# Fifteen up-projection chunks by seven products instead of seven: weight sums on GpSimd, two of four low parts by adding DMAs, the next chunk's first product as filler

## The chip, the cores and the metric

The kernel runs on one core of a Trainium2 chip, in one launch. The metric is the device time of that launch in microseconds (us); lower is better. A core has five engines with a queue of instructions each: TensorE (PE, matmuls; its weight loads are listed as PEld), VectorE (DVE), ScalarE (ACT), GpSimd (POOL) and SyncE (SP, which here only issues DMAs). They run at the same time and wait for one another by semaphores; each works its own queue off in program order. DMAs are issued from the queues of SP and of POOL and are carried out by 16 DMA engines. SBUF is the on-chip memory of 128 partitions; PSUM holds the results of matmuls in eight banks of 128 x 512 float32.

## What is computed

The reference is a trunk of two decoder layers over a stream h of 512 tokens by 1024 features, all in float32. Each layer is an attention and then a gated feed-forward part with a short causal convolution, each between two RMS norms. The change is in the feed-forward part, which both layers have:

```python
def conv_ffn(xn, w_up, cw, cb, w_down):          # xn (1, 512, 1024), w_up (1024, 5632)
    a = xn @ w_up
    T = a.shape[1]
    ap = jnp.pad(a, ((0, 0), (CONV_W - 1, 0), (0, 0)))
    a = sum(ap[:, j:j + T] * cw[j] for j in range(CONV_W)) + cb
    gate, val = jnp.split(a, 2, axis=-1)
    return (jax.nn.gelu(gate, approximate=True) * val) @ w_down
...
        f = conv_ffn(rms_norm(h, g[2]), w_up[l], conv_w[l], conv_b[l], w_down[l])
        h = h + rms_norm(f, g[3])
```

## The kernel before

**Precision.** Every float32 operand is split into a high part (ScalarE copies it into the matmul format float32r) and a low part (what is left, by VectorE's subtraction). A product of two operands is then three matmuls: high x high, high x low, low x high (`mm3`, lines 263 to 265). The low part of a weight is made in one of two ways: by VectorE, `raw - high` (line 62), or by an adding DMA: ScalarE also writes the negated raw (line 56) and a DMA from POOL's queue adds the raw to it (line 77, `accum_op=ALU.add`).

**The up-projection.** `ffn(l, ...)` runs once per layer. The 5632 columns of w_up are taken in 22 chunks; chunk c has 128 columns of the gate and 128 of the value. A plain chunk (`up`) multiplies each of the two by x, transposed (xT, 1024 features by 512 tokens), in 8 steps of 128 features: 2 x 8 x 3 = 48 matmuls of 512 columns. Their results stand in two PSUM banks. `taps` then applies the convolution (ScalarE's Identity, line 592, and two VectorE instructions, lines 593 and 595, for each bank) into a tile bb, `glu` the gelu of the gate (line 613), `product` the product of the two (line 610) into hc, which a DMA from POOL's queue writes to DRAM (line 608).

**Seven products.** The chunks in SEVEN (6, 8, ..., 18) use a scheme in the manner of Strassen and Winograd on a 2 x 2 split: the features in two halves, the tokens in two halves (LO, HI), the gate and the value as the other two. Four weight blocks a11, a12, a21, a22 of 4 x 128 x 128 give the operands A11, A12, A22 and the sums S1 = a21 + a22, S2 = S1 - a11, S3 = a11 - a21, S4 = a12 - S2; sums of the blocks of x (XA, XB) are made once per layer by `sums_in` (line 627 on GpSimd). Seven products of 12 matmuls of 256 columns each, 84 in all, go into the four halves o1 to o4 of the two banks: A11 into o1, S2 into o2, S3 into o3, A12 into o1, S1 into o2, A22 into o3, and S4 into o2. Between them ScalarE copies o1 (s1, line 900) and VectorE makes s12 = o2 + s1 and s17 = o3 + s1 (lines 902, 903), o4 = o2 + s17 (910), o3 += s12 (915) and at the end o2 += s1 (917). Two accesses to one PSUM bank are kept in order even where they touch different halves. The first half of the next, plain chunk stands between A22 and S4.

**Its weights.** `seven_weights(c + 2)` runs as a generator, a step at a time, during chunk c: it takes two raw tiles r0 and r1, makes the four sums on VectorE (lines 656 to 661), four casts on ScalarE (655, 660, 664, 667) and four low parts on VectorE (663, 666, 669, 671).

**What sets the order.** The order in each engine's queue is the program order of the text (`manual_schedule`); nothing is reordered. Tiles come from pools: p8 (16 tiles of 8 KB per partition: operands), p4 (10 of 4 KB: raw weights wraw, weight sums wsum, bb, one gain), p2 (8 of 2 KB: csum, hc) and the eight PSUM banks. The first write into a new tile waits until the last access to the old tile in the same place is done, so a pool also sets when transfers start. `W.load` issues the raw loads on SP's queue (line 46); `W.take` hands raw tiles out, `W.get` gives split ones.

Of the kernel before, what the change touches and what calls it, by code (L numbers as in the profile page):

```python
# [15 lines left out]
T = 512  # L16
# [7 lines left out]
BIG = 3.0e38  # L24


SEVEN = range(6, 19, 2)
ND = NF // 2
LAST = 3

# [66 lines left out]
def trunk_kernel(ctx, tc, x, norm_gains, w_qkv_a, w_o_a, w_q_b, w_o_b, kv_norm, w_kvf, b_f,  # L97
# [164 lines left out]
    def mm3(o, ah, al, bh, bl, first, last, shared=False):  # L262
        pe.matmul(o, ah, bh, start=first, stop=False, skip_group_check=shared)  # L263
        pe.matmul(o, ah, bl, start=False, stop=False, skip_group_check=shared)  # L264
        pe.matmul(o, al, bh, start=False, stop=last, skip_group_check=shared)  # L265
# [317 lines left out]
    def ffn(l, bd, cp, nxt, ahead):  # L583
        hD = tc.dram_tile([NF, 128, T], F32, name="hD")
        sD = tc.dram_tile([ND, 128, 256], F32, name="sD")
        hc = {}

        def taps(c, banks, between=None):
            bb = t4([128, 2, T], name="bb")
            for s, ch in ((0, c), (1, NF + c)):  # L590
                ps = banks[s]
                act.activation(bb[:, s, :], ps, AF.Identity, bias=cp[:, 3, ch:ch + 1], scale=cp[:, 2, ch:ch + 1])  # L592
                dve.scalar_tensor_tensor(bb[:, s, 1:], ps[:, :T - 1], cp[:, 1, ch:ch + 1], bb[:, s, 1:],  # L593
                                         ALU.mult, ALU.add)
                dve.scalar_tensor_tensor(bb[:, s, 2:], ps[:, :T - 2], cp[:, 0, ch:ch + 1], bb[:, s, 2:],  # L595
                                         ALU.mult, ALU.add)
                if s == 0 and between is not None:
                    between()
            return bb

        gated = []
# [1 line left out]
        def product():  # L603

            if gated:
                c, bb = gated.pop()
                if c - 1 in hc:
                    pool.dma_start(hD[c - 1], hc.pop(c - 1))  # L608
                hc[c] = t2([128, T], name="hc")
                dve.tensor_tensor(hc[c], bb[:, 0, :], bb[:, 1, :], ALU.mult)  # L610

        def glu(c, bb):
            act.activation(bb[:, 0, :], bb[:, 0, :], AF.Gelu_apprx_tanh)
            gated.append((c, bb))
# [26 lines left out]

        halves = {}

        def split_pair(pair, src, n=1024):
            act.copy(pair[:, 0, :n], src)
            yield
            dve.tensor_tensor(pair[:, 1, :n], src, pair[:, 0, :n].bitcast(F32), ALU.subtract)

        def seven_weights(c):

            r0, r1 = W.take(2)
            w = [t8([128, 2, 1024], F32R, name="w") for _ in range(4)]
            sa, sb = (t4([128, 1024], name="wsum") for _ in range(2))
            a11, a12, a21, a22 = r0[:, 0:512], r0[:, 512:1024], r1[:, 0:512], r1[:, 512:1024]
            act.copy(w[0][:, 0], r0)
            dve.tensor_tensor(sa[:, 0:512], a11, a21, ALU.subtract)
            dve.tensor_tensor(sb[:, 0:512], a21, a22, ALU.add)
            yield
            dve.tensor_tensor(sa[:, 512:1024], sb[:, 0:512], a11, ALU.subtract)
            act.copy(w[1][:, 0], sa)  # L660
            dve.tensor_tensor(sb[:, 512:1024], a12, sa[:, 512:1024], ALU.subtract)
            yield
            dve.tensor_tensor(w[1][:, 1], sa, w[1][:, 0].bitcast(F32), ALU.subtract)
            act.copy(w[2][:, 0], sb)
            yield
            dve.tensor_tensor(w[0][:, 1], r0, w[0][:, 0].bitcast(F32), ALU.subtract)
            act.copy(w[3][:, 0, 0:512], a22)
            yield
            dve.tensor_tensor(w[2][:, 1], sb, w[2][:, 0].bitcast(F32), ALU.subtract)
            yield  # L670
            dve.tensor_tensor(w[3][:, 1, 0:512], a22, w[3][:, 0, 0:512].bitcast(F32), ALU.subtract)
            v = [t.rearrange("p s (q k c) -> p s q k c", q=2, k=4) for t in w]
            halves[c] = dict(A11=v[0][:, :, 0], A12=v[0][:, :, 1], S3=v[1][:, :, 0], S2=v[1][:, :, 1],
                             S1=v[2][:, :, 0], S4=v[2][:, :, 1], A22=v[3][:, :, 0])
# [10 lines left out]
        def weights(c):  # L685
            return seven_weights(c) if c in SEVEN else plain_weights(c)

# [184 lines left out]
        W.ahead = 1  # L872
        W.split(base + 8)
        extra = sums_in()
        begun = None
        before = None
        for c in range(2, NF):
            if c == NF - 4:
                pair_load(0)
            if c == NF - 3:  # L880
                sums = down_sums([(l, ND - 1), (1, 8 + l)], in_one, pool, 1, 0)
                next(sums)
            steps = weights(c + 2) if c + 2 < NF else iter(())
            banks = [bank([128, T], name="up") for _ in range(2)]
            if c in SEVEN:
                w = halves.pop(c)
                W.n_get += 2
                x11, x21, x22 = [(xT[0][i], xT[1][i], s) for i, s in ((0, LO), (1, LO), (1, HI))]
                o1, o2, o3, o4 = banks[0][:, LO], banks[0][:, HI], banks[1][:, LO], banks[1][:, HI]
                s1, s12, s17 = (t2([128, 256], name="csum") for _ in range(3))  # L890

                def prod(o, a, x, start=False):
                    half_mm(o, w[a], x[0:2], x[2], start)

                prod(o1, "A11", x11, True)
# [4 lines left out]
                act.copy(s1, o1)  # L900
                next(steps)
                dve.tensor_tensor(s12, o2, s1, ALU.add)
# [12 lines left out]
                dve.tensor_tensor(o3, o3, s12, ALU.add)  # L915
                next(steps, None)
                dve.tensor_tensor(o2, o2, s1, ALU.add)  # L917
            else:
                for s in range(2):
                    if s == 0 and begun:  # L920
                        w, banks[0] = begun
                        up(*begun, range(4, KD))
                        begun = None
                    else:
                        up(W.get(), banks[s], range(KD))
                    if c == NF - 2:
                        next(sums)
                    if s == 0 and before:
# [4 lines left out]
                    next(steps, None)  # L933
                    next(extra, None)
            run(steps)
            before = c, banks
            if c == NF - 3:
                pair_sums(0)
        post(*before, lambda: pair_lows(1))
# [719 lines left out]
```

## Time and profile before

| what | us |
|---|---|
| median of 3 runs | 1129.99 (1129.57 to 1130.77) |
| span of the profiled execution, first to last instruction | 1125.8 |
| TensorE busy in the span | 1114.3 |
| VectorE busy | 893.8 |
| ScalarE busy | 616.5 |
| GpSimd busy | 191.6 |

The profile gives the span of one execution and no time of its own beside it; the runs are timed from outside. A line of a group of instructions reads: line, engine, operation, output<-inputs, shapes, number; after the bar the busy time and the mean duration of one in ns; after the second bar how long the engine stood idle before them and what ended it. A line of the timeline reads: start and duration in us, engine, line, operation, tiles, how many were merged, and in brackets the idle time before. A queue's row gives packets, megabytes and the time of its packets as a share of 16 DMA engines in that window. PE busy is not TensorE at its peak, since matmuls overlap; the spacing of their starts tells the rate.

### The profile page before, as it was taken

What the parts mean: (1) busy time and instruction counts of PE and PEld (TensorE: products, weight loads), DVE (VectorE), ACT (ScalarE), POOL (GpSimd) and SP (SyncE); (2) the same over time, 40 slices, a digit from 0 to 9 for tenths busy, and PEclk for the clock granted to TensorE, in tenths of its full rate; (3) what the DMA queues carried; (4) which work ended last, traced back from release to release, by engine and by line L of the source; (5) the groups of instructions that cost most, each with busy time, mean ns of one, the idle gap of its engine ahead of it and who ended that gap; (6) DMA issues with size and microseconds to landing.
All of it is one profiled execution on the core that took longest, in us unless ns stands there. A gap on an engine that the chain in (4) does not pass through costs nothing. (4 is left out here: it accounts for less than half of the span.)

```text
span 1125.8 us, 17268 instructions
## 1 busy us (share of the span) xinstructions
PE 1114.3 (99%) x6267; PEld 950.6 (84%) x6267; DVE 893.8 (79%) x1449; ACT 616.5 (55%) x1038; POOL 191.6 (17%) x291
## 2 busy tenths in 40 slices
PE   9999999999999999999999999999999999999997
PEld 6988889889899888888778888789989989988886
DVE  6668778888888689997588677847888788689894
ACT  5454565545444456576562588746444454456572
POOL 1832101200000121000000556600400000121000
PEclk9999999999999999999999999999999999999999
DMA  9469854333443699793447766473334343499861
GB/s 322 150 222 407 320 161 133 94 119 106 142 123 115 160 346 370 293 333 100 128 151 253 235 168 160 123 209 107 118 94 122 115 138 122 138 351 368 326 243 75
DMA packets 179471, 218.38 MB, mean 194 GB/s; under 512 B 11257, under 2 KB 131049, under 8 KB 179386
## 3 DMA queue, kind: packets, MB, share of 16 engines
q1 hardware_dynamic: 168634, 180.84, 49.0%
q0 software_dynamic: 10752, 36.45, 10.5%
q8 instruction: 49, 0.80, 0.3%
q14 instruction: 36, 0.29, 0.1%
HBM read 166.08 MB, written 39.63 MB: 183 GB/s over the span
## 5 line engine op out<-in xcount | busy, mean ns | idle before, releaser
L592 ACT ACTIVATE bb<-up,conv 128x512 f32<-128x512 f32 x80 | 60.6, 775 | 149.5 <-DVE up L917 76.2
L62 DVE TENSOR_TENSOR w<-wraw,w 128x1024 fp32r<-128x1024 f32 x96 | 123.0, 1312 | 22.1 <-ACT w L54 21.6
L54 ACT CAST w<-wraw 128x1024 fp32r<-128x1024 f32 x110 | 111.6, 1047 | 19.4 <-PE v_ps L264 11.6
L263 PE MATMUL acc<-w 128*128 128x512 f32 (+1 forms) x311 | 120.7, 388 | 1.1 <-DVE mix L310 1.1
L265 PE MATMUL acc<-w 128*128 128x512 f32 (+1 forms) x311 | 120.6, 388 | 0.0
L263 PE MATMUL up<-xch,w 128*128 128x512 f32 (+1 forms) x292 | 104.9, 359 | 0.0
L264 PE MATMUL up<-xcl,w 128*128 128x512 f32 (+1 forms) x292 | 104.9, 359 | 0.0
L263 PE MATMUL up<-xbh,w 128*128 128x512 f32 (+1 forms) x292 | 104.9, 359 | 0.0
L264 PE MATMUL up<-xbl,w 128*128 128x512 f32 (+1 forms) x292 | 104.9, 359 | 0.0
L265 PE MATMUL up<-xbh,w 128*128 128x512 f32 (+1 forms) x292 | 104.8, 359 | 0.0
L265 PE MATMUL up<-xch,w 128*128 128x512 f32 (+1 forms) x292 | 104.8, 359 | 0.0
L264 PE MATMUL acc<-w 128*128 128x512 f32 (+1 forms) x267 | 103.3, 387 | 0.0
L608 POOL DMA_DIRECT2D hD<-hc x42 | 24.2, 576 | 316.9 <-DVE hc L610 316.6
L263 PEld LDWEIGHTS acc<-w 128*128 128x128 f32 x311 | 58.4, 188 | 13.1 <-DVE mix L310 1.3
L265 PEld LDWEIGHTS acc<-w 128*128 128x128 f32 x311 | 58.4, 188 | 12.1 <-DVE w L720 0.3
L593 DVE SCALAR_TENSOR_TENSOR bb<-up,conv,bb 128x511 f32<-128x511 f32 x80 | 59.5, 744 | 7.7 <-ACT bb L592 7.7
L265 PE MATMUL up<-xsh,w 128*128 128x256 f32 x224 | 63.5, 283 | 0.0
L264 PE MATMUL up<-xsl,w 128*128 128x256 f32 x224 | 63.5, 283 | 0.0
L263 PE MATMUL up<-xsh,w 128*128 128x256 f32 x224 | 63.5, 283 | 0.0
L595 DVE SCALAR_TENSOR_TENSOR bb<-up,conv,bb 128x510 f32<-128x510 f32 x80 | 59.9, 749 | 2.8
L263 PEld LDWEIGHTS up<-xbh,w 128*128 128x128 f32 x292 | 55.1, 189 | 8.3
L263 PEld LDWEIGHTS up<-xch,w 128*128 128x128 f32 x292 | 55.1, 189 | 8.2
(303 smaller groups left out, 3040.7 us busy)
## 6 DMA issues: line engine op xcount, KB each, us to landing
wraw<-in_w_up_dram SPq DMA_DIRECT2D x88, 512.0 KB, 4.7
dT<-dsums SPq DMA_DIRECT2D x24, 512.0 KB, 6.5
dsums<-in_w_down_dram SPq DMA_DIRECT2D x22, 512.0 KB, 7.2
dsums<-in_w_down_dram SPq DMA_DIRECT2D x44, 256.0 KB, 6.6
hD<-hc POOLq DMA_DIRECT2D x44, 256.0 KB, 4.7
dact<-hD SPq DMA_DIRECT2D x44, 256.0 KB, 6.2
wraw<-dT SPq DMA_DIRECT2D x22, 512.0 KB, 9.9
wraw<-in_w_down_dram SPq DMA_DIRECT2D x22, 512.0 KB, 6.3
```

The costliest lines, as they stand in the source:

```text
L54: self.nc.scalar.copy(pair[:, 0], raw)
L62: self.nc.vector.tensor_tensor(pair[:, 1], raw, pair[:, 0].bitcast(F32), ALU.subtract)
L263: pe.matmul(o, ah, bh, start=first, stop=False, skip_group_check=shared)
L264: pe.matmul(o, ah, bl, start=False, stop=False, skip_group_check=shared)
L265: pe.matmul(o, al, bh, start=False, stop=last, skip_group_check=shared)
L592: act.activation(bb[:, s, :], ps, AF.Identity, bias=cp[:, 3, ch:ch + 1], scale=cp[:, 2, ch:ch + 1])
L593: dve.scalar_tensor_tensor(bb[:, s, 1:], ps[:, :T - 1], cp[:, 1, ch:ch + 1], bb[:, s, 1:], ALU.mult, ALU.add)
L595: dve.scalar_tensor_tensor(bb[:, s, 2:], ps[:, :T - 2], cp[:, 0, ch:ch + 1], bb[:, s, 2:], ALU.mult, ALU.add)
L608: pool.dma_start(hD[c - 1], hc.pop(c - 1))
```

## The change

SEVEN becomes 4 to 18, every chunk. The weight sums go to GpSimd (`sums_of`, which forms S1 in place of a21). Of the four pairs of operands, two (wA of a11 and a12, wC of S3 and S2) get their low parts by adding DMAs (`added`), in `split_first` at the end of chunk c for c + 2; the other two (wB of S1 and a22, w4 of S4) by VectorE as before, in `split_rest` during chunk c for c + 1. w4 now is a p4 tile, and S4's sum a p2 tile. A11 of chunk c + 1 (`begin`) stands between A22 and S4. The taps of the gate of chunk c are moved into chunk c + 1 (`finish`), those of the value are at the end of chunk c. Raw weights are loaded for c + 3 after `product`.

```diff
--- before.py
+++ after.py
@@ -24,7 +24,7 @@
 BIG = 3.0e38
-SEVEN = range(6, 19, 2)
+SEVEN = range(4, 19)
 ND = NF // 2
 LAST = 3
@@ -585,17 +585,24 @@
         sD = tc.dram_tile([ND, 128, 256], F32, name="sD")
         hc = {}
...
         def taps(c, banks, between=None):
-            bb = t4([128, 2, T], name="bb")
...
+            bb = new_bb()
+            tap(c, 0, banks[0], bb)
+            if between is not None:
+                between()
+            tap(c, 1, banks[1], bb)
             return bb
...
         gated = []
@@ -641,37 +648,42 @@
         halves = {}
-        def split_pair(pair, src, n=1024):
-            act.copy(pair[:, 0, :n], src)
+        def sums_of(c):
+            r0, r1 = W.take(2)
+            sc, s4 = t4([128, 1024], name="wsum"), t2([128, 512], name="wsum4")
+            a11, a12, a21, a22 = r0[:, 0:512], r0[:, 512:1024], r1[:, 0:512], r1[:, 512:1024]
+            s3, s2 = sc[:, 0:512], sc[:, 512:1024]
+            pool.tensor_tensor(s3, a11, a21, ALU.subtract)
+            pool.tensor_tensor(a21, a21, a22, ALU.add)
+            pool.tensor_tensor(s2, a21, a11, ALU.subtract)
+            pool.tensor_tensor(s4, a12, s2, ALU.subtract)
+            made[c] = r0, r1, sc, s4
+        def added(raw, name):
+            w = t8([128, 2, 1024], F32R, name=name)
+            act.copy(w[:, 0], raw)
+            act.activation(w[:, 1], raw, AF.Copy, scale=-1.0)
+            pool.dma_start(w[:, 1], raw, accum_op=ALU.add)
+            return w
+        def split_first(c):
+            r0, r1, sc, s4 = made[c]
+            made[c] = r1, s4, added(r0, "wA"), added(sc, "wC")
+        def split_rest(c):
+            r1, s4, wa, wc = made.pop(c)
+            wb, w4 = t8([128, 2, 1024], F32R, name="wB"), t4([128, 2, 512], F32R, name="w4")
+            act.copy(wb[:, 0], r1)
+            act.copy(w4[:, 0], s4)
             yield
-            dve.tensor_tensor(pair[:, 1, :n], src, pair[:, 0, :n].bitcast(F32), ALU.subtract)
-        def seven_weights(c):
...
+            dve.tensor_tensor(wb[:, 1], r1, wb[:, 0].bitcast(F32), ALU.subtract)
+            dve.tensor_tensor(w4[:, 1], s4, w4[:, 0].bitcast(F32), ALU.subtract)
+            q = [[t[:, p].rearrange("p (q k c) -> p q k c", k=4, c=128) for p in range(2)] for t in (wa, wb, wc, w4)]
+            halves[c] = {key: [t[:, i] for t in q[m]] for key, m, i in (
+                ("A11", 0, 0), ("A12", 0, 1), ("S1", 1, 0), ("A22", 1, 1), ("S3", 2, 0), ("S2", 2, 1), ("S4", 3, 0))}
+        made = {}
...
@@ -856,7 +865,7 @@
         def half_mm(o, w, x, s, start):
             for k in range(4):
-                mm3(o, w[:, 0, k, :], w[:, 1, k, :], x[0][:, k, s], x[1][:, k, s], start and k == 0, k == 3, True)
+                mm3(o, w[0][:, k, :], w[1][:, k, :], x[0][:, k, s], x[1][:, k, s], start and k == 0, k == 3, True)
         def up(w, o, kcs):
             wh, wl = (t.rearrange("p (k c) -> p k c", k=8) for t in w)
@@ -872,68 +881,121 @@
         W.ahead = 1
         W.split(base + 8)
         extra = sums_in()
+        next(extra)
+        x11, x21, x22 = [(xT[0][i], xT[1][i], q) for i, q in ((0, LO), (1, LO), (1, HI))]
         begun = None
         before = None
+        finish = None
+        def begin(c):
+            b = bank([128, T], name="up")
+            half_mm(b[:, LO], halves[c]["A11"], x11[0:2], x11[2], True)
+            return b
         for c in range(2, NF):
+            W.ahead_dma = 0 if c + 2 in SEVEN else 2
             if c == NF - 4:
                 pair_load(0)
             if c == NF - 3:
                 sums = down_sums([(l, ND - 1), (1, 8 + l)], in_one, pool, 1, 0)
                 next(sums)
-            steps = weights(c + 2) if c + 2 < NF else iter(())
-            banks = [bank([128, T], name="up") for _ in range(2)]
+            later = c + 2
+            plain = plain_weights(later) if later < NF and later not in SEVEN else iter(())
+            rest = split_rest(c + 1) if c + 1 in SEVEN else iter(())
             if c in SEVEN:
+                gate, value = begun or begin(c), bank([128, T], name="up")
+                begun = None
                 w = halves.pop(c)
                 W.n_get += 2
-                x11, x21, x22 = [(xT[0][i], xT[1][i], s) for i, s in ((0, LO), (1, LO), (1, HI))]
-                o1, o2, o3, o4 = banks[0][:, LO], banks[0][:, HI], banks[1][:, LO], banks[1][:, HI]
-                s1, s12, s17 = (t2([128, 256], name="csum") for _ in range(3))
+                o1, o2, o3, o4 = gate[:, LO], gate[:, HI], value[:, LO], value[:, HI]
+                s1, s12_17 = t2([128, 256], name="csum"), t2([128, 2, 256], name="csum")
+                s12, s17 = s12_17[:, 0], s12_17[:, 1]
                 def prod(o, a, x, start=False):
                     half_mm(o, w[a], x[0:2], x[2], start)
-                prod(o1, "A11", x11, True)
                 prod(o2, "S2", (*XB, HI))
                 prod(o3, "S3", (*XA, HI), True)
-                product()
-                bb = taps(*before)
                 act.copy(s1, o1)
-                next(steps)
-                dve.tensor_tensor(s12, o2, s1, ALU.add)
+                def sum_two():
+                    dve.tensor_tensor(s12, o2, s1, ALU.add)
+                if later in SEVEN:
+                    sums_of(later)
+                if finish is not None:
+                    finish(sum_two)
+                    bb = before[1]
+                else:
+                    product()
+                    sum_two()
+                    bb = taps(*before)
+                next(rest, None)
                 dve.tensor_tensor(s17, o3, s1, ALU.add)
-                glu(before[0], bb)
+                next(rest, None)
+                next(plain, None)
                 prod(o1, "A12", x21)
                 prod(o2, "S1", (*XA, LO))
                 prod(o3, "A22", (*XB, LO))
-                next(steps)
-                next(steps, None)
+                product()
+                W.load(W.n_split + 2)
+                glu(before[0], bb)
                 dve.tensor_tensor(o4, o2, s17, ALU.add)
-                begun = W.get(), bank([128, T], name="up")
-                up(*begun, range(4))
+                if c + 1 in SEVEN:
+                    begun = begin(c + 1)
+                else:
+                    begun = W.get(), bank([128, T], name="up")
+                    up(*begun, range(4))
                 prod(o2, "S4", x22)
-                next(steps, None)
+                if later in SEVEN:
+                    split_first(later)
+                next(plain, None)
                 dve.tensor_tensor(o3, o3, s12, ALU.add)
-                next(steps, None)
-                dve.tensor_tensor(o2, o2, s1, ALU.add)
+                bb = new_bb()
+                tap(c, 1, value, bb)
+                def finish(between=None, c=c, gate=gate, s1=s1, bb=bb):
+                    dve.tensor_tensor(gate[:, HI], gate[:, HI], s1, ALU.add)
+                    tap(c, 0, gate, bb, between)
+                before = c, bb
             else:
...
+                    if s == 0 and finish is not None:
+                        finish()
+                        product()
+                        glu(*before)
+                        finish = None
...
+                    if s == 0 and later in SEVEN:
+                        sums_of(later)
+                    if s == 1 and later in SEVEN:
+                        split_first(later)
+                    next(rest, None)
+                    next(plain, None)
...
```

More of the change, by code (lines that the diff above doesn't have):

```diff
@@ L586, in ffn, with tap, new_bb @@
         hc = {}
-        def taps(c, banks, between=None):
-            bb = t4([128, 2, T], name="bb")
[L590 to L598, printed above, removed]
+        def tap(c, s, ps, bb, between=None):
+            ch = c + s * NF
+            act.activation(bb[:, s, :], ps, AF.Identity, bias=cp[:, 3, ch:ch + 1], scale=cp[:, 2, ch:ch + 1])
+            if between is not None:
+                between()
+            for d, r in ((1, 1), (2, 0)):
+                dve.scalar_tensor_tensor(bb[:, s, d:], ps[:, :T - d], cp[:, r, ch:ch + 1], bb[:, s, d:],
+                                         ALU.mult, ALU.add)
+        def new_bb():
+            return t4([128, 2, T], name="bb")
+        def taps(c, banks, between=None):
+            bb = new_bb()
+            tap(c, 0, banks[0], bb)
+            if between is not None:
+                between()
+            tap(c, 1, banks[1], bb)
             return bb
@@ L642, in ffn @@
         halves = {}
-        def split_pair(pair, src, n=1024):
-            act.copy(pair[:, 0, :n], src)
-            yield
-            dve.tensor_tensor(pair[:, 1, :n], src, pair[:, 0, :n].bitcast(F32), ALU.subtract)
-        def seven_weights(c):
[L651 to L674, printed above, removed]
@@ L927, in ffn @@
                         next(sums)
[L928 removed]
+                    if s == 0 and finish is not None:
[3 more added lines that the diff above has]
+                        finish = None
+                        if c >= NF - 2:
+                            pair_highs(c - NF + 2)
+                            pair_sums(c - NF + 3)
+                    elif s == 0 and before:
                         post(*before, (lambda: pair_lows(0)) if c == NF - 1 else None)
@@ L932, in ffn @@
                             pair_sums(c - NF + 3)
-                    next(steps, None)
+                    if s == 0 and later in SEVEN:
[4 more added lines that the diff above has]
+                    next(plain, None)
                     next(extra, None)
-            run(steps)
-            before = c, banks
+                    next(extra, None)
+                before = c, banks
+            run(rest)
+            run(plain)
             if c == NF - 3:
```

4 lines of the change are left out of this document (2 added, 2 removed).

## The prediction

> **What bounds the kernel now.** I read the busy times first, then one stretch of the up-projections, then the spacing of its matmuls.
>
> ```profile
> span 1125.8 us, 17268 instructions
> PE 1114.3 (99%) x6267; PEld 950.6 (84%) x6267; DVE 893.8 (79%) x1449; ACT 616.5 (55%) x1038; POOL 191.6 (17%) x291
> ```
> TensorE is busy in 99% of the span. The span is 1125.8 us and the median of the runs 1129.99, so 4.2 us lie around it; I add differences to the median.
>
> ```profile
> core 0: us, PE busy (x) PEld busy (x) DVE busy (x) ACT busy (x) POOL busy (x), PEclk, DMA share, GB/s
> 855.00:876.00 21.00, 21.00 (x134) 19.09 (x133) 17.72 (x26) 9.79 (x13) 1.08 (x2) 1.00 0.42 127
> ```
> One pair of chunks (one by seven products, one plain) takes 21.00 us, all of it TensorE at full clock. VectorE is busy 17.72, ScalarE 9.79, GpSimd 1.08, and the DMA engines 42%.
>
> ```profile
> 860.68 0.39 PE L263 MATMUL up<-xch,w 128*128 128x512 f32 x1
> 866.12 0.28 PE L263 MATMUL up<-xch,w 128*128 128x256 f32 x1
> 867.55 0.28 PE L263 MATMUL up<-xsh,w 128*128 128x256 f32 x1
> ```
> These are the first matmul of a plain half chunk, of product A11 and of S2. A half chunk (24 matmuls of 512 columns) issues in 866.12 - 860.68 = 5.44 us, a product (12 of 256) in 1.43. A plain chunk is thus 10.88 and seven products 10.01; the 0.11 left of 21.00 I split evenly: 10.94 and 10.06. Each conversion saves **0.87 us** of TensorE time, not the eighth that the count of multiplications suggests, since a matmul of half the width takes 0.119 against 0.227.
>
> **The change on TensorE.** Chunks 4, 5, 7, 9, 11, 13, 15 and 17 are converted, eight in each of two layers: 16 x 0.87 = 13.9 us. That is all that can be won, and only where nothing else takes over 10.06 us per chunk. The fifteen chunks 4 to 18 now take 7 x 10.06 + 8 x 10.94 = 157.9 us per layer, 10.53 each: above that the change loses.
>
> **Work of the other engines per converted chunk.**
>
> ```profile
> L592 ACT ACTIVATE bb<-up,conv 128x512 f32<-128x512 f32 x80 | 60.6, 775 | 149.5 <-DVE up L917 76.2 <-PE up L265 73.3
> L593 DVE SCALAR_TENSOR_TENSOR bb<-up,conv,bb 128x511 f32<-128x511 f32 x80 | 59.5, 744 | 7.7 <-ACT bb L592 7.7
> L610 DVE TENSOR_TENSOR hc<-bb 128x512 f32<-128x512 f32 x44 | 30.1, 685 | 0.8 <-ACT bb L613 0.8
> L613 ACT ACTIVATE bb<-bb 128x512 f32<-128x512 f32 x44 | 27.7, 630 | 26.0 <-DVE bb L595 26.0
> L663 DVE TENSOR_TENSOR w<-wsum,w 128x1024 fp32r<-128x1024 f32 x14 | 17.2, 1225 | 4.7 <-ACT w L660 4.7
> L660 ACT CAST w<-wsum 128x1024 fp32r<-128x1024 f32 x14 | 14.7, 1050 | 12.0 <-DVE wsum L659 12.0
> L56 ACT ACTIVATE w<-wraw 128x1024 fp32r<-128x1024 f32 x14 | 14.9, 1061 | 0.0
> L741 ACT CAST w<-dt 128x512 fp32r<-128x512 f32 x22 | 13.6, 618 | 5.9 <-DMA dt<-dT 5.9
> L608 POOL DMA_DIRECT2D hD<-hc x42 | 24.2, 576 | 316.9 <-DVE hc L610 316.6 <-DMA w<-wraw 0.2
> ```
> ```profile
> 869.19 0.37 ACT L900 COPY csum<-up 128x256 f32<-128x256 f32 x1 [2.10 <-PE up L265]
> 869.87 0.42 DVE L902 TENSOR_TENSOR csum<-up,csum 128x256 f32<-128x256 f32 x1
> ```
> ScalarE: two Identity 1.55, a gelu 0.63, s1 0.37, three wide casts 3.15, two negated copies 2.12 and one narrow cast 0.62, together 8.4 us against 9.79 per pair. VectorE: four taps 2.98, the product 0.69, five sums of 256 columns 2.1, two low parts 1.92 (1.225 and, as the 128x512 product, 0.69), together 7.7. Both lie under 10.06 if they needn't wait. The moved filler costs nothing: A11 of the next chunk gives TensorE 1.43 us while VectorE makes o4 (0.42) after A22, where four steps of the plain chunk stood.
>
> GpSimd gets the four weight sums, whose price no row shows at this size:
>
> ```profile
> 193.69 10.20 POOL L627 TENSOR_TENSOR xsum<-xbh,xbl 128x2048 f32<-128x2048 f32 x2 [52.29 <-DVE xbl L335]
> 194.35 5.05 DVE L62 TENSOR_TENSOR w<-wraw,w 128x1024 fp32r<-128x1024 f32 x1
> 199.36 0.75 DVE L593 SCALAR_TENSOR_TENSOR bb<-first,conv,bb 128x511 f32<-128x511 f32 x1
> L627 POOL TENSOR_TENSOR xsum<-xbh,xbl x2: 4626/5124/5622, 193.7 to 198.3; 128x2048 f32<-128x2048 f32 x2
> ```
> The undisturbed sum of 2048 columns took 4.63 us; a quarter is 1.16, which I take (bounds: 0.69, VectorE's own, and 1.41, a quarter of the disturbed one). Four are 4.6 us; with hD's issue 0.58 and two adding DMAs at 0.89 GpSimd has 7.0 us. The same rows show a cost: the low part L62 took 5.05 us instead of 1.22 since it ended only after GpSimd's instruction at 198.3 had, and GpSimd's next one then took 1.0 longer. The taps, which read PSUM, kept 0.75. So VectorE's product and two low parts may each wait up to 1.16 us. I count 0: 2.4 us are free in VectorE's 10.06, and their readers come late in the chunk; without that cover it is up to 3.5 a chunk. The Trainium skill, "SBUF — State Buffer", section Who interferes with whom, says that a VectorE instruction with two SBUF inputs and a GpSimd instruction that reads SBUF exclude each other for a whole instruction. By that rule the sum could grow by the 3.5, without it by nothing; the 5.05 agrees with it.
>
> **The DMA engines.**
>
> ```profile
> q1 hardware_dynamic: 8390, 4.23, 35.1%
> q0 software_dynamic: 320, 1.05, 6.2%
> ```
> ```profile
> q0 software_dynamic: 156, 0.54, 51.4%
> ```
> ```profile
> 386.00:396.00 10.00, 10.00 (x51) 8.49 (x51) 6.29 (x12) 5.04 (x7) 0.77 (x1) 1.00 1.04 291
> ```
> The first two rows are the queues from 855 to 897 us: eight raw loads and four hD writes. A load takes 0.351 x 42 / 8 = 1.84 us of all 16 engines, hD 0.65. The third is one adding DMA in the attention phase (692.18 to 697.60): 0.514 x 5.42 = 2.79. A converted chunk needs 2 x 1.84 + 2 x 2.79 + 0.65 = **9.9 us of 10.06**, 2.36 MB. The last row shows full engines moving 291 GB/s; 2.36 MB in 10.06 us are 235, of which nearly half is of the slow adding kind. So the engines are all but full, and transfers queue.
>
> ```profile
> L77 POOL DMA_DIRECT2D w<-wraw x6: 916/926/932, 640.1 to 704.8; - x6
> DMA to landing us min/median/max: 5.3/5.9/7.4
> ```
> ```profile
> L77 POOL DMA_DIRECT2D w<-wraw x4: 845/855/899, 382.4 to 397.1; - x4
> DMA to landing us min/median/max: 8.3/9.0/9.9
> ```
> ```profile
> L46 SPq DMA_DIRECT2D wraw<-in_w_up_dram x8: 367/368/368, 857.0 to 895.0; - x8
> DMA to landing us min/median/max: 4.2/4.8/5.4
> ```
> An adding DMA lands 5.9 us after its issue (median) in the attention phase, but 8.3 to 9.9 in pairs on the full engines of 382 to 397 us.
>
> **The waits that the change adds.** They come from the ten p4 tiles:
>
> ```profile
> 876.76 1.21 DVE L669 TENSOR_TENSOR w<-wsum,w 128x1024 fp32r<-128x1024 f32 x1
> 878.00 0.37 SPq L46 DMA_DIRECT2D wraw<-in_w_up_dram  x1
> ```
> The load at 878.00 starts when L669, the last reader of an old weight sum, ends at 877.97: it takes over that tile. A tile passes on in the order in which the old ones have had their last use. Per chunk c the new loop takes five (the sum for c+2, w4 of c+1, two raws of c+3, bb) and gives back five in this order: second raw of c+1, bb, w4 of c, then first raw and sum of c+2, both last read by the adding DMAs. One tile is a gain, six are held when a chunk begins, so the three given back last are taken first. Hence w4 of c+1 gets the first raw of c+1, and **ScalarE's cast into w4 waits for the landing of the adding DMA of c+1**, issued a chunk earlier; behind it in ScalarE's queue stand gelu, the next copies and the next adding DMA. And the first raw of c+3 gets the sum of c+1, so SP's load waits for the other adding DMA.
>
> Loop A, each chunk: landing, w4 cast 0.62, gelu 0.63, high part 1.05, negated 1.06, issue of the next adding DMA. With 5.9 it is 9.3 us, with 8.3 it is **11.7**. Loop B, every second chunk: landing of the second adding DMA, two loads (4.8 + 1.84), four sums 4.6, hD 0.58, issue 0.89. With 5.9 it is 18.6, 9.3 a chunk; with 9.0 it is 21.7, 10.9 a chunk. I take 11.7, the slower, with the row of pairs on full engines, since the new loop fills them at any period near 10.06 (at 11.7 still to 85%). 15 x 11.7 = 175.5, which is 17.6 over 157.9. At the start (chunks 2 to 4) GpSimd does xsum (10.2 us) and two sets of sums, and bb waits for an adding DMA: between 0 and one landing more, 8.3; I take 3. Two layers: 2 x 20.6 = 41, so **1171 us**. With loop A's landing between 7.3 and 9.0 (10.7 to 12.4 a chunk) it is 1140 to 1191.
>
> **Rivals.** 1: *TensorE stays the bound.* If adding DMAs land within 10.06 - 3.36 = 6.7 us and loop B stays under 20.1, every wait is hidden and the gain is 13.9: 1116. For it: 5.9 in the attention phase, both loops at 9.3. Against it: 9.9 of 10.06. It decides at that 6.7. With the start's 3 us per layer it is 1122. Chance 0.15.
>
> 2: *The raw loads starve.* In the queue rows a load has some 1000 packets and an adding DMA 150, so if the engines alternate by packets, the adding DMAs land in 5.9 but loads wait behind both (2 x 2.79): loop B is 5.9 + 6.64 + 5.58 + 6.07 = 24.2, 12.1 a chunk, +23.6 per layer, and with the start 1183; with GpSimd's waits added up to 1205. Chance 0.22. The Trainium skill, "DMA: Bandwidth & Descriptors", section Queues, rings and completion order, says that an engine goes round its queues packet by packet. No run here shows loads against adding DMAs, so I keep it as the second case.
>
> 3: *The queues just fit.* Landings of 6.7 to 7.3 give 10.06 to 10.66 a chunk, with the start 1122 to 1140. Chance 0.13: 0.06 faster, 0.04 within 0.2% (about what a measurement of this kernel can tell from no change), 0.03 slower.
>
> **Numbers.** Forecast 0.50, rivals 0.15, 0.22 and 0.13. Faster 0.15 + 0.06 = 0.21, same 0.04, slower 0.50 + 0.22 + 0.03 = 0.75. The range 1122 to 1205 leaves out rival 1 and little above rival 2.
>
> **What would show it.** Starts of S2 in successive chunks: 11 to 12.5 us apart, not 10.06. ScalarE's cast into w4 waiting for a DMA out of wraw; SP's loads waiting for DMAs out of wsum; GpSimd's first sum waiting for wraw; TensorE below 97%; DMA share in this stage above 0.8 instead of 0.42; adding DMAs landing in 8 us. Wrong would be: landings under 6.7 with S2 10.06 apart, a TensorE that waits for VectorE's low parts behind GpSimd (the lock, not the tiles), or w4 free long before its cast.

## The result and the profile after

| kernel | median, us | runs | ratio to before, 95% interval |
|---|---|---|---|
| before | 1129.78 (1127.55 to 1130.77) | 4 | |
| changed | 1167.94 (1166.32 to 1168.89) | 4 | 1.0338 (1.0325 to 1.0351) |

The changed kernel is 38.2 us slower. Its profiled execution took 1168.23 us with a span of 1166.4. The first two lines of its page, the span and the busy times:

```profile
span 1166.4 us, 18950 instructions
PE 1116.4 (96%) x6843; PEld 971.9 (83%) x6843; DVE 918.7 (79%) x1445; ACT 703.4 (60%) x1146; POOL 435.5 (37%) x471
```

TensorE's busy sum is about that of before (1114.3), and its idle time is 50 us instead of 11.5. The busy sum doesn't show the work that the conversions save: the same matmuls add up to 1105.4 us in w4_in_8 below, where TensorE waits less. Where that idle time lies is told by the windows of four stages: the up-projection and the down-projection of layer 0, then of layer 1, cut at TensorE's first and last matmul of each. Before:

```profile
core 0: us, PE busy (x) PEld busy (x) DVE busy (x) ACT busy (x) POOL busy (x), PEclk, DMA share, GB/s
206.93:419.25 212.32, 212.32 (x1215) 187.72 (x1214) 172.90 (x239) 102.80 (x132) 17.50 (x30) 1.00 0.49 152
419.25:520.00 100.75, 100.75 (x445) 83.26 (x444) 93.75 (x126) 67.35 (x89) 5.38 (x10) 1.00 0.83 293
801.57:1013.88 212.31, 212.31 (x1214) 187.72 (x1213) 173.93 (x240) 102.78 (x132) 17.52 (x30) 1.00 0.50 153
1013.88:1120.30 106.42, 105.25 (x472) 87.22 (x470) 91.76 (x130) 63.26 (x86) 5.38 (x10) 1.00 0.72 261
```

The same four of the changed kernel:

```profile
208.65:438.23 229.58, 211.78 (x1502) 197.56 (x1501) 184.16 (x236) 146.04 (x186) 137.56 (x119) 1.00 0.83 214
438.23:540.40 102.17, 100.92 (x445) 83.21 (x444) 95.02 (x128) 67.81 (x89) 5.41 (x11) 1.00 0.81 287
823.08:1052.37 229.29, 213.15 (x1502) 198.95 (x1501) 180.88 (x235) 145.93 (x186) 137.80 (x119) 0.99 0.83 213
1052.37:1160.94 108.57, 105.62 (x472) 87.10 (x470) 94.56 (x133) 63.27 (x87) 5.39 (x10) 1.00 0.71 257
```

The up-projections lose 17.3 and 17.0 us; TensorE stands idle there for 17.8 and 16.1 us, and before for none. The down-projections, which the diff doesn't touch, lose 1.4 and 2.2. The rest of the two spans' difference of 40.6 us lies in a later start (1.7) and in the attention between.

The copy s1 (line 920) comes once a chunk. Its first and last start in layer 0, for chunks 4 and 18:

```profile
234.46 0.34 ACT L920 COPY csum<-up 128x256 f32<-128x256 f32 x1
398.34 0.37 ACT L920 COPY csum<-up 128x256 f32<-128x256 f32 x1 [0.94 <-PE up L265]
```

That is 163.88 / 14 = **11.71 us a chunk**; in layer 1 it is 11.69. "Chunk" below is this spacing, as a mean over both layers. The waits of the changed kernel, the engine and line that waited, what for, and in total, times and longest in us (first SP's queue, then the others):

```profile
SPq L46 <- DMA wC<-wsum: 281.2, 28, 19.8
SPq L46 <- DMA wA<-wraw: 49.8, 4, 16.6
```
```profile
POOL wsum L657 <- DMA wraw<-in_w_up_dram: 45.8, 18, 3.9
ACT w L678 <- DMA wA<-wraw: 43.6, 25, 3.4
PEld up L263 <- DVE up L944: 26.1, 25, 1.8
DVE csum L923 <- DMA hD<-hc: 23.4, 17, 2.7
POOL wA L667 <- ACT wA L666: 21.1, 5, 8.3
PE up L263 <- DVE up L944: 21.0, 25, 1.6
PE up L263 <- DVE csum L923: 12.1, 19, 2.3
```

The waits forecast are there: raw loads behind adding DMAs (28 times for wC), GpSimd's first sum (657) behind raw loads, ScalarE's cast of w4 (678) behind wA. One is new: s12 (923) takes over a 2 KB tile, hc, whose write to DRAM is under way. TensorE in the end waits for VectorE's o4 and s12. The issues, with the median from issue to landing (of the raw loads, the profile has a landing for 20 of the 88):

```profile
wraw<-in_w_up_dram SPq DMA_DIRECT2D x88, 512.0 KB, 4.8
wA<-wraw POOLq DMA_DIRECT2D x30, 512.0 KB, 7.5
wC<-wsum POOLq DMA_DIRECT2D x30, 512.0 KB, 8.9
```

Two rows of ScalarE, its w4 casts in successive chunks, and the issue of wA by GpSimd between them:

```profile
913.40 0.62 ACT L678 CAST w<-wsum 128x512 fp32r<-128x512 f32 x1 [3.19 <-DMA wA<-wraw]
924.62 0.62 ACT L678 CAST w<-wsum 128x512 fp32r<-128x512 f32 x1 [1.96 <-DMA wA<-wraw]
```
```profile
909.56 1.26 POOL L657 TENSOR_TENSOR wsum<-wraw 128x512 f32<-128x512 f32 x1 [3.38 <-DMA wraw<-in_w_up_dram]
910.90 1.29 POOL L658 TENSOR_TENSOR wraw<-wraw 128x512 f32<-128x512 f32 x1
912.27 2.32 POOL L659 TENSOR_TENSOR wsum<-wraw 128x512 f32<-128x512 f32 x1
914.67 1.63 POOL L660 TENSOR_TENSOR wsum<-wraw,wsum 128x512 f32<-128x512 f32 x1
916.25 0.61 POOL L615 DMA_DIRECT2D hD<-hc  x1
916.85 0.89 POOL L667 DMA_DIRECT2D wA<-wraw  x1
```

This is loop A closing: from one cast to the next 11.22 us, of which 7.77 from wA's issue at 916.85. But that issue stands right behind GpSimd's hD, and GpSimd was late because its first sum waited 3.38 us for a raw tile. So loop B (raw loads) sets when wA is issued in loop A. The waits say how often: only 5 of 30 issues of wA waited for ScalarE's negated copy (666); most found it done.

### The profile page after: what moved, and what is told of

It reads as the page before. It is cut to its first block, busy times and chain, and to the rows that moved or that the text cites. A ratio compares the mean times of both kernels' runs of the same rounds, so it can differ in the third digit from the quotient of the medians.

```text
span 1166.4 us, 18950 instructions
## 1 busy us (share of the span) xinstructions
PE 1116.4 (96%) x6843; PEld 971.9 (83%) x6843; DVE 918.7 (79%) x1445; ACT 703.4 (60%) x1146; POOL 435.5 (37%) x471
## 5 line engine op out<-in xcount | busy, mean ns | idle before, releaser
L594 DVE SCALAR_TENSOR_TENSOR bb<-up,conv,bb 128x511 f32<-128x511 f32 (+1 forms) x160 | 119.1, 748 | 37.6 <-ACT bb L590 34.6
L62 DVE TENSOR_TENSOR w<-wraw,w 128x1024 fp32r<-128x1024 f32 x64 | 85.4, 1361 | 18.5 <-ACT w L54 18.0
L265 PEld LDWEIGHTS acc<-w 128*128 128x128 f32 x311 | 58.4, 188 | 15.6 <-DVE w L729 3.8
L263 PE MATMUL up<-xsh,wB 128*128 128x256 f32 x240 | 68.7, 286 | 0.9 <-DVE csum L935 0.9
L263 PEld LDWEIGHTS acc<-w 128*128 128x128 f32 x311 | 58.4, 188 | 13.0 <-DVE mix L310 1.3
L264 PE MATMUL up<-xsl,wB 128*128 128x256 f32 x240 | 68.4, 285 | 0.0
L265 PE MATMUL up<-xsh,wB 128*128 128x256 f32 x240 | 68.3, 285 | 0.0
L263 PE MATMUL up<-xsh,wC 128*128 128x256 f32 x240 | 67.9, 283 | 0.0
L264 PE MATMUL up<-xsl,wC 128*128 128x256 f32 x240 | 67.9, 283 | 0.0
L265 PE MATMUL up<-xsh,wC 128*128 128x256 f32 x240 | 67.8, 283 | 0.0
L657 POOL TENSOR_TENSOR wsum<-wraw 128x512 f32<-128x512 f32 x30 | 39.8, 1328 | 64.3 <-DMA wraw<-in_w_up_dram 45.8
L263 PE MATMUL up<-xbh,w 128*128 128x512 f32 (+1 forms) x140 | 49.4, 353 | 11.9 <-DVE up L944 11.9
L264 PEld LDWEIGHTS acc<-w 128*128 128x128 f32 x267 | 50.1, 188 | 10.5 <-DVE w L729 0.2
L263 PE MATMUL up<-xch,w 128*128 128x512 f32 (+1 forms) x140 | 49.3, 352 | 9.1 <-DVE up L944 9.1
L659 POOL TENSOR_TENSOR wsum<-wraw 128x512 f32<-128x512 f32 x30 | 56.8, 1895 | 2.3
```

Source lines behind the costliest of these rows:

```text
L62: self.nc.vector.tensor_tensor(pair[:, 1], raw, pair[:, 0].bitcast(F32), ALU.subtract)
L594: dve.scalar_tensor_tensor(bb[:, s, d:], ps[:, :T - d], cp[:, r, ch:ch + 1], bb[:, s, d:], ALU.mult, ALU.add)
L657: pool.tensor_tensor(s3, a11, a21, ALU.subtract)
L659: pool.tensor_tensor(s2, a21, a11, ALU.subtract)
```

## The experiments

Theory: the hand-over of the 4 KB tiles ties raw loads and the w4 cast to adding DMAs. Rivals: the lock between GpSimd and VectorE (instructions of one grow long beside those of the other); DMA engines that can't do the work; the wait of s12 for hD. Which tile takes over which follows from the addresses that the tiles get.

| kernel | chunk, us | median, us | ratio to before (95%) |
|---|---|---|---|
| changed | 11.70 | 1167.94 | 1.0338 (1.0325 to 1.0351) |
| fifteen | 11.72 | 1181.14 | 1.0452 (1.0423 to 1.0482) |
| p4_11 | 10.76 | 1149.87 | 1.0181 (1.0149 to 1.0214) |
| p2_10 | 11.88 | 1179.69 | 1.0441 (1.0415 to 1.0467) |
| p4_12 | 10.25 | 1135.51 | 1.0055 (1.0038 to 1.0072) |
| before_gain | | 1129.56 | 1.0003 (0.9993 to 1.0013) |
| gain_late | 10.49 | 1140.64 | 1.0097 (1.0073 to 1.0120) |
| one_add | 11.02 | 1146.66 | 1.0159 (1.0142 to 1.0176) |
| gain_no_add | 13.5 (layer 0) | 1220.41 | 1.0810 (1.0790 to 1.0831) |
| w4_in_8 | 10.25 | 1129.75 | 1.0004 (0.9993 to 1.0016) |
| gain_w4_in_8 | 10.25 | 1128.95 | 1.0000 (0.9990 to 1.0010) |
| w8_wait | 10.86 | 1146.60 | 1.0155 (1.0138 to 1.0172) |
| w8_sums_dve | 12.27 | 1182.97 | 1.0477 (1.0463 to 1.0490) |

### More tiles of one kind: fifteen, p4_11, p2_10, p4_12

So that no memory is added, one 8 KB tile is given up for one or two of 4 KB or two of 2 KB; fifteen, which only gives the tile up, is the control.

```diff
-    p8 = ctx.enter_context(tc.tile_pool(name="p8", bufs=16))
-    p4 = ctx.enter_context(tc.tile_pool(name="p4", bufs=10))
-    p2 = ctx.enter_context(tc.tile_pool(name="p2", bufs=8))
+    p8 = ctx.enter_context(tc.tile_pool(name="p8", bufs=15))     # all four
+    p4 = ctx.enter_context(tc.tile_pool(name="p4", bufs=11))     # p4_11 (p4_12: 12)
+    p2 = ctx.enter_context(tc.tile_pool(name="p2", bufs=10))     # p2_10
```

> The changed kernel with 15 of the 8 KB tiles in place of 16, nothing else: the control for the next three, which need that memory. The tiles of 4 KB and 2 KB keep their hand-overs. Every theory: the changed kernel's time, 1168 us, within 4 us.

> 15 of the 8 KB tiles and 11 tiles of 4 KB in place of 10. The cast of w4 now takes over the w4 of two chunks before, which TensorE has long read, and no longer the raw tile that the adding DMA wA reads; the raw loads still take over tiles that wA and wC of the chunk before read. Theory (the hand-over of 4 KB tiles ties the steps to landings): loop A is gone, loop B of 10.9 us a chunk stays, so 30 chunks x 0.8 us = 24 us less, 1144 us (1135 to 1155). Rival lock (GpSimd and VectorE in each other's way, sums of 1.3 to 2.3 us for 1.16): 1160 to 1168. Rival DMA engines (share 0.85 at 11.7 us a chunk, so 9.9 us of work): landings grow as the chunk shortens, 1150 to 1165. Rival hD (the sum s12 waits for the write of hc): 1160 to 1168.

> 15 of the 8 KB tiles and 10 tiles of 2 KB in place of 8: s12 no longer takes over the hc tile whose write to hD is under way; the copy s1 takes over an older one. Theory (4 KB tiles): loops A and B are as they were, 1163 to 1168. Rival hD: VectorE's wait of 23.4 us (17 waits) before s12 goes, and with it 15 to 23 us, 1145 to 1153. Rivals lock and DMA engines: 1163 to 1168.

> 15 of the 8 KB tiles and 12 tiles of 4 KB. w4 takes over an old bb; one raw tile takes over an old w4, the other the raw that wA reads; no raw waits for wC, but bb takes over the wsum that wC reads, a chunk later. Theory (4 KB tiles): both loops are cut to wA's landing alone, 10.1 to 10.6 us a chunk, 1120 to 1140. Rival lock: 1155 to 1168. Rival DMA engines: 1145 to 1165, with landings of 10 us and more. Rival hD: 1160 to 1168.

The control missed: one 8 KB tile less costs 13 us, though the chunk stays at 11.72. It is lost in other stages (the second layer's up-projection begins at 829.72 instead of 823.08), so the three are compared with fifteen. p4_11 takes 31.3 us off, p4_12 45.6. p2_10 takes 1.4, within the intervals, though in its waits s12 no longer stands behind hD: that wait was not what set the period, and rival hD falls. In layer 1 of p4_12 all periods but the first are 10.08 to 10.25. A window there:

```profile
850.00:970.00 120.00, 120.00 (x1001) 119.88 (x1001) 96.19 (x144) 90.85 (x119) 88.02 (x82) 1.00 1.08 239
```

TensorE is busy without a gap, with both adding DMAs, with the sums on GpSimd, and with the DMA engines moving 239 GB/s. So neither the engines nor the lock kept the changed kernel at 11.7 by themselves; the tiles did. The landings did move, some up and some down: here raw loads took 7.0 us instead of 4.8, and wA 5.7 instead of 7.5.

```profile
wraw<-in_w_up_dram SPq DMA_DIRECT2D x88, 512.0 KB, 7.0
wA<-wraw POOLq DMA_DIRECT2D x30, 512.0 KB, 5.7
```

### The same without giving up memory: before_gain, gain_late

One 4 KB tile holds the gain row of the next norm all through the chunks. It can be loaded at their end:

```diff
-    bd2 = SharedBoundary(load_gain(norm_gains[0, 3], "gain03"), gcol, "xk")
+    bd2 = SharedBoundary(lambda: load_gain(norm_gains[0, 3], "gain03"), gcol, "xk")
...
+        nxt.mix.gain = nxt.mix.gain()
         down(nxt, ahead)
```

> The kernel before, with the load of the gain row for the end of each down-projection moved from ahead of the up-projections to their end; it frees one 4 KB tile during the chunks. The control for the next kernels that use this. The chunks of before wait for no such tile: 1129 us, within 3 us, by every theory.

> The changed kernel with the gain row loaded at the end of the up-projections: one 4 KB tile more for the chunks, at 16 of the 8 KB tiles, and by it the hand-overs of p4_11 (w4 takes over an old w4, both raws wait for the adding DMAs wA and wC of the chunk before). Theory (4 KB tiles): p4_11 was 31 us under its control, so 1168 - 31 = 1137 us (1131 to 1142), at 10.7 us a chunk; loop B of 10.9 is what is left. If p4_11's gain hung on the 8 KB tiles' order instead: 1155 to 1168.

Both as the theory had them (1140.64 in the stated range; before unmoved). gain_late is loop B without A: no cast of w4 waits, but SP's loads still do, and GpSimd's first sum too. It is not quite the changed kernel's loop B: there SP's loads wait mostly for wC (28 times, against 4 for wA), here for wA and for wC.

```profile
SPq L46 <- DMA wA<-wraw: 230.5, 30, 18.4
SPq L46 <- DMA wC<-wsum: 58.5, 26, 4.0
```
```profile
POOL wsum L657 <- DMA wraw<-in_w_up_dram: 22.9, 17, 2.5
```

### Fewer adding DMAs: one_add, gain_no_add

```diff
-            made[c] = r1, s4, added(r0, "wA"), added(sc, "wC")
+            wa, wc = added(r0, "wA"), t8([128, 2, 1024], F32R, name="wC")
+            act.copy(wc[:, 0], sc)
+            dve.tensor_tensor(wc[:, 1], sc, wc[:, 0].bitcast(F32), ALU.subtract)
+            made[c] = r1, s4, wa, wc
```

gain_no_add makes both low parts so, on top of gain_late.

> The changed kernel with the low part of wC subtracted by VectorE, so that one adding DMA (wA) and one negated copy a chunk are left; no memory is added. By the new order of releases w4 takes over an old w4, the sum an old sum, one raw tile the raw that wA reads, the other a raw read by VectorE. Theory (4 KB tiles): loop A gone, and of loop B one raw's wait for wA: 10.1 to 10.3 us a chunk, 1168 - 30 x 1.5 = 1122 us (1116 to 1130), though VectorE gets 1.05 us a chunk more (7.7 to 8.8). Rival lock or VectorE (sums of GpSimd and lows of VectorE in each other's way decide): 1145 to 1170. If the landing of the raws' tie still decides: 1137, as gain_late.

> gain_late with both low parts, of wA and wC, subtracted by VectorE: no adding DMA, no negated copy, no tile waits for a landing; VectorE at 7.7 + 2.1 = 9.8 us a chunk of 10.08. If VectorE's work and its lock with GpSimd don't bind: 1116 to 1125, and the adding DMAs were not needed. If they do: 10.5 to 11 us a chunk, 1130 to 1145.

Both missed the theory. one_add's 1146.66 lies in the range of its rival, lock or VectorE, and the first chunks show it at work. Past the first, the chunks are 10.4 us, near the forecast, but the first of each layer takes 18.9 and 19.2. In layer 0, VectorE still makes low parts of the sums of x there, and the next four instructions ahead of s12 (the low parts of wC, wB and w4, and the product) take 8.4 us beside GpSimd's sums, where their undisturbed times add up to 3.8. So s12 is late, and TensorE waits in one piece:

```profile
PE up L263 <- DVE csum L926: 7.6, 1, 7.6
```

Twice 7.6 is most of the 17 us over w4_in_8 below. In gain_no_add the price is every chunk's. VectorE's timeline, with the two low parts (666) that took the adding DMAs' place:

```profile
913.71 2.29 DVE L666 TENSOR_TENSOR wA<-wraw,wA 128x1024 fp32r<-128x1024 f32 x1
915.92 2.31 DVE L666 TENSOR_TENSOR wC<-wsum,wC 128x1024 fp32r<-128x1024 f32 x1
918.15 0.42 DVE L953 TENSOR_TENSOR up<-up,csum 128x256 f32<-128x256 f32 x1
919.48 1.53 DVE L594 SCALAR_TENSOR_TENSOR bb<-up,conv,bb 128x511 f32<-128x511 f32 x2 [0.91 <-ACT bb L590]
```

They fall on GpSimd's sums and take 2.3 us each for 1.22, so VectorE has 4.6 us and not 2.4 more, ahead of o3 (953) and the taps in its queue. GpSimd's first sum waits 6.7 us there for VectorE's product, which puts the sums beside the low parts. So the adding DMAs pay in this order of the program; another order wasn't tried.

### No memory, one word: w4_in_8, gain_w4_in_8

```diff
-            wb, w4 = t8([128, 2, 1024], F32R, name="wB"), t4([128, 2, 512], F32R, name="w4")
+            wb, w4 = t8([128, 2, 1024], F32R, name="wB"), t8([128, 2, 512], F32R, name="w4")
```

> The changed kernel with the tile w4 taken from the 8 KB tiles in place of the 4 KB ones, nothing else: no memory is added, 16 tiles of 8 KB stay. By the order of releases the hand-overs become those of p4_12: no w4 and only one of the two raws waits for an adding DMA (wA). Theory (4 KB tiles): the chunk goes to 10.08 us as in p4_12, without what 15 tiles cost (1181 - 1168 = 13 us): 1135.5 - 13 = 1122 us (1118 to 1126). Rival: two more of the 8 KB tiles in use cost what the missing one did: 1130 to 1137.

> w4_in_8 with the gain row loaded late as well: no raw waits for any adding DMA; bb waits for wA and the sum of a chunk for wC of the chunk before. Theory: if TensorE is the bound at 10.08 us a chunk already, nothing is left to gain: 1122 us, within 3 us of w4_in_8. If the one wait for wA still costs at the layer's start: 2 to 6 us less than w4_in_8.

Every engine's instructions are those of the changed kernel, in the same order; only tiles lie elsewhere. It is 38.2 us faster than it. The chunks are the forecast's: two rows of s1 in layer 0,

```profile
234.58 0.35 ACT L920 COPY csum<-up 128x256 f32<-128x256 f32 x1
377.45 0.37 ACT L920 COPY csum<-up 128x256 f32<-128x256 f32 x1 [1.03 <-PE up L265]
```

give 142.87 / 14 = 10.20, and all but the first two periods there are 10.08. Yet the time is before's, 1129.75, not 1122. Its four stages:

```profile
208.77:417.23 208.46, 206.67 (x1502) 196.50 (x1501) 165.24 (x236) 145.02 (x186) 124.01 (x119) 1.00 0.92 235
417.23:519.80 102.57, 100.92 (x445) 83.20 (x444) 95.41 (x128) 67.67 (x89) 5.62 (x11) 1.00 0.81 287
802.30:1012.00 209.70, 206.93 (x1503) 196.55 (x1501) 166.37 (x235) 144.80 (x186) 123.96 (x119) 1.00 0.92 233
1012.00:1120.80 108.80, 105.82 (x472) 87.10 (x470) 94.55 (x133) 63.60 (x87) 5.40 (x10) 1.00 0.71 257
```

The up-projections take 3.9 and 2.6 us less than before, not 7 each as forecast. TensorE's busy time fell by 5.7 and 5.4 there, and it now waits 1.8 and 2.8, all of it at the start of the seven-product chunks (o4, s12 and s17 late on VectorE). The down-projections give back 1.8 and 2.4. Their wait, in layer 1:

```profile
PE acc L265 <- DVE w L729: 1.8, 1, 1.8
PE acc L263 <- DVE mix L310: 1.1, 1, 1.1
```

The second line is in the kernel before too; the first isn't: the up-projections end sooner and VectorE's low parts for the first products of the down-projection come late. What is left, a start of the up-projections that is 1.8 us later and 0.9 in the attention between them, lies where no instruction was changed; in the single profiles of all the kernels here that start lies between 206.55 and 209.66, so 1.8 us of it can't be put down to a cause. gain_w4_in_8, in which no cast of w4 and only one raw load a layer waits for an adding DMA, is the same within the intervals, and its chunk is 10.25 too, although wA lands in 7.9 us there and wC in 9.2. What costs is not a long landing but a tile that hangs on it, and the 4 KB tiles have nothing left to give. No version here beats the kernel before by more than a measurement can tell.

### Loop A alone, and the lock: w8_wait, w8_sums_dve

```diff
+            act.copy(w4[:, 0, 0:1], wa[:, 1, 0:1])
             act.copy(w4[:, 0], s4)
```

> w4_in_8 with one copy of a single element per chunk on ScalarE, from the low part of wA into w4 ahead of the cast of w4 (which overwrites it): the cast waits for the landing of wA again, as by the tile of the changed kernel, while the raws are as in w4_in_8. It is loop A alone. Theory as predicted (loop A is 11.7 us by itself): 30 chunks x 1.6 us over w4_in_8, so 1165 to 1172. If loops A and B share the loss (p4_11, loop B alone, left 0.5 to 0.9 us a chunk): 1140 to 1155. If loop A costs nothing when raws come early: 1120 to 1128.

In w8_sums_dve the four sums are issued by VectorE at the same place of the program.

> w4_in_8 with the four weight sums of a chunk on VectorE in place of GpSimd. VectorE gets 4 x 0.69 = 2.8 us a chunk more, 7.7 + 2.8 = 10.5 of 10.08, but GpSimd is no longer in its way (the sums took 1.3 to 2.3 us on GpSimd, and VectorE's own operations up to 1.8 for 0.7). If VectorE's busy time decides: 10.5 to 10.9 us a chunk, 1135 to 1150. If the lock costs as much as the work: 1120 to 1128, as w4_in_8.

w8_wait is 16.9 us over w4_in_8, the middle case: loop A alone costs 0.61 us a chunk. Three of its waits:

```profile
POOL wA L667 <- ACT wA L666: 47.5, 24, 8.6
ACT w L678 <- DMA wA<-wraw: 34.0, 25, 3.0
```
```profile
POOL wsum L657 <- DMA wraw<-in_w_up_dram: 1.7, 2, 0.9
```

The first is in w4_in_8 too (46.8 us, 25 times); the second, of ScalarE's cast for wA, is what the edit added; and by the third, raw loads hardly hold up the sums.

w8_sums_dve went beyond both ranges, to 12.27 us a chunk. The lock is gone: the low part of wB (680), whose median in w4_in_8 is 1884 ns, takes 1214 to 1218 in all 30 chunks (min, median, max in ns; w4_in_8, then w8_sums_dve):

```profile
L680 DVE TENSOR_TENSOR wB<-wraw,wB x30: 1215/1884/2344, 232.2 to 965.0; 128x1024 fp32r<-128x1024 f32 x30
```
```profile
L680 DVE TENSOR_TENSOR wB<-wraw,wB x30: 1214/1215/1218, 229.1 to 1018.5; 128x1024 fp32r<-128x1024 f32 x30
```

But the 2.8 us of sums now stand ahead of o2, s12 and the taps in VectorE's queue, and TensorE waits 42.1 us for s12 in 26 chunks. VectorE is busy only 95.27 of 120 us (860 to 980), so its order seems to decide, not its sum; no run moved the sums within its queue. At this place of the program, GpSimd was the better engine for them.

## Why the prediction was right, and where its steps were not

**TensorE's floor and the break-even: right.** 10.06 us were forecast for a chunk with no waits, 10.08 were measured.

**The mechanism: right.** Cutting the hand-over of the 4 KB tiles, with every instruction unchanged, takes the whole 38.2 us away (w4_in_8). The wait of the cast alone, put back by one small copy, brings 16.9 of them back (w8_wait).

**Loop A at 11.7 and "the slower of the two" loops: wrong in the working, right in the period.** wA landed in 7.5 us, not 8.3; with that the formula gives 7.5 + 3.36 = 10.86, and loop A alone did measure 10.86, though with wA landing in 6.9 there, so the agreement is partly luck. That 11.7 was forecast from loop A alone, and 11.70 came from both loops together, is luck too. Loop B alone was 10.49 (forecast 10.9). Over the 10.25 of w4_in_8 they cost 0.61 and 0.24, but together 1.45. They are not two separate circles of which the slower counts. As the rows from 909 to 925 us have it, a late raw makes the sums late, the sums stand ahead of wA's issue in GpSimd's queue, and the late wA holds up the w4 cast and with it ScalarE, which has to make the next wA. In times: 16.9 for A, 11.7 for B (gain_late over gain_w4_in_8), 38.2 for both. The parts aren't exact, since gain_late's loads wait for other landings than the changed kernel's; that both together cost more than the larger holds with a wide margin.

**Landings from full DMA engines: wrong as a ground.** I took 8.3 because 9.9 us of engine work in 10.06 would fill them. With that work at 10.25 us a chunk, wA landed in 5.7 (p4_12), 6.5 (w4_in_8) and 7.9 (gain_w4_in_8), wC in 7.4, 8.2 and 9.2, and raw loads in 7.0, 5.6 and 5.8. So some transfers did come later than before, but full engines didn't tell which: at the same period 8.3 would have been near in one kernel and far off in another. p4_12's share of 1.08 is above what engines can be busy, so the packet times that it adds up must overlap.

**The start and the end.** 3 us a layer were taken for the start. The first period is 11.7 in the changed kernel, and about 11.7 in w4_in_8 too, so the start's 1.6 us is there without a wait of the cast. The up-projections lost 17.3 and 17.0 us, what was forecast for the loop alone (17.6), so the 3 is not to be found there. Not forecast were 1.4 and 2.2 us in the down-projections. That 17.3 + 1.4 and 17.0 + 2.2 per layer come near 20.6 is luck again.

**The lock at 0: right with cover, wrong without.** Without the tile waits the sums on GpSimd cost TensorE nothing past the first chunks of a layer (p4_12, w4_in_8). In the changed kernel the third sum (659) took 2.16 us in the median, against 1.30 in w4_in_8, and lies in the joined loop, so it made that longer. How much of the 38 us it adds wasn't measured by itself. The prediction gave a TensorE that waits for VectorE behind GpSimd as a sign of being wrong, and TensorE did wait for o4 and s12. But the narrow low part of w4 (681) shows which comes first (changed kernel, then w4_in_8):

```profile
L681 DVE TENSOR_TENSOR w<-wsum,w x30: 684/1782/1795, 233.2 to 1006.4; 128x512 fp32r<-128x512 f32 x30
```
```profile
L681 DVE TENSOR_TENSOR w<-wsum,w x30: 678/679/1797, 233.4 to 966.1; 128x512 fp32r<-128x512 f32 x30
```

With the same instructions in the same order it is long in 26 chunks of 30 and in 4: what GpSimd's sums fall on is set by the tile waits. The Trainium skill, "SBUF — State Buffer", section Who interferes with whom, has the rule, a whole instruction's exclusion; 1782 against 684 ns agrees with it, and each of the 26 lay beside a sum of GpSimd.

**The moved filler at 0: right where VectorE isn't late.** TensorE waited 21.0 us for o4 in 25 chunks of the changed kernel, and 1.9 in 2 of w4_in_8.

**The rivals.** TensorE as the bound was to need landings under 6.7; 7.5 and 8.9 were measured, and it didn't come. But 6.7 was not the divide: in gain_w4_in_8 TensorE is the bound with landings of 7.9 and 9.2. Even so the time is 1129 and not 1116 to 1122: the 13.9 us were TensorE's share of the chunks alone, and 8.8 of them went in waits at the start of the chunks and in the next stage (w4_in_8). Starving raw loads: in the changed kernel they landed in 4.8 us in the median, as before. In p4_12 they did come late beside the adding DMAs, in 7.0, at no cost to TensorE in the window from 850 to 970. The prediction says that no run showed loads against adding DMAs; its own pairs from 382 to 398 us did, with SP's queue at 56.1% and POOL's at 37.0% of the engines, and there the adding DMAs landed in 9.0 and not in the 5.9 that this rival takes. Its upper end of 1205 was given without a sum. Queues that just fit (1122 to 1140) fell with the period of 11.70.

## What to carry to other kernels

When a DMA reads a tile, the tile's place is busy until the DMA has landed: list for each pool which old tile every new one takes over, since moving one tile to another pool was worth 38 us here with no instruction changed. Two loops that shared a queue didn't cost the larger of the two here; cut each alone and both to see what they make together. A long landing costs only what hangs on it. And before a faster stage is counted as a gain, see what the first instructions of the next stage wait for.

## What the runs showed of the hardware

The DMA share of a window went to 1.08 at 239 GB/s, so in this view it is no occupancy. wA landed sooner there than in the changed kernel (5.7 us for 7.5) and raw loads later (7.0 for 4.8): the share didn't tell which transfers come late. A GpSimd sum of 128x512 took 1.26 to 1.30 us undisturbed (1.16 was scaled from a longer one) and up to 2.36 beside VectorE in the changed kernel; VectorE's low part of 128x512 took 0.68 and up to 1.80 beside GpSimd.
